# A decoder block on one core: low parts on GpSimd, two banks for the value products, scratch by key square

## The chip, the core and the metric

The kernel runs on one core of a Trainium2 chip. The core's engines work at the same time, each through its own instructions in order: TensorE (PE) multiplies matrices into the PSUM banks, with its weight loads listed apart as PEld; VectorE (DVE) and ScalarE (ACT) work on tiles in SBUF and PSUM; GpSimd (POOL) works on tiles in SBUF and issues DMAs; SyncE (SP) only issues DMAs here. Semaphores order what depends on each other. The metric is the device time of one execution in microseconds.

## The reference

One layer over 512 positions of 1024 channels, in float32. A combined projection of the normalized input gives a short gated convolution (mixer A), the queries, keys and values of an attention with three branches (mixer B), and two gates per channel:

```python
h = rmsnorm(x, norm1_g[l]); proj = h @ w_in[l]
y_a = a_b * causal_dwconv(a_c * a_x, conv_a_w[l])
y_b = nsa(q, k_cmp, v_cmp, k_sel, v_sel, k_win, v_win, gates)   # 8 heads of 64, 2 key groups
gm = jax.nn.sigmoid(g_merge)
mix = gm[..., :D_MODEL] * (y_a @ w_a_out[l]) + gm[..., D_MODEL:] * (y_b @ w_b_out[l])
x = x + mix @ w_o[l]
h = rmsnorm(x, norm2_g[l]); gu = h @ w_ffn_in[l]
g = causal_dwconv(gu[..., :D_FF], ffn_conv_w[l]) + ffn_conv_b[l]
x = x + (jax.nn.silu(g) * gu[..., D_FF:]) @ w_ffn_out[l]
```

The attention adds three softmax products, each with its gate: over 31 compressed keys, over selected key blocks, and over a window. There are 8 blocks of 64 keys and 16 may be selected, so all causal keys are; the window of 512 holds all of them too. So the selected and the window branch are both plain causal attention, each with keys and values of its own.

## The kernel before

**High and low parts.** The products have float32 accuracy out of operands of a shorter type (`F32R`): a value v becomes a high part h, which ScalarE writes by a copy (`split`, L157; the probabilities' own in L719), and a low part v - h. A product of two split operands is three matmuls: high by high, high by low, low by high. `dense` (L412 to L418) runs them over the tiles of 128 channels. The low part comes from VectorE (L158, L720), from GpSimd (L140, for the gate weights and the output weights of mixer A), or from a DMA that adds the raw weight to minus the high part (`dma_split`, L161 to L165).

**Stages.** The projections per token and the compression of keys and values come first; then attention (`attend`, L606) and, beside it, the work of mixer A (`conv_tile`, L752), the gates (`gate_tile`, L775) and mixer A's output (`mix_a_pair`, L784). Then come mixer B's output `pmb` (L838 to L851), the output projection (L876) and the feed-forward part with its down products (`ff_pair`, `down_part`).

**The order.** The program text is not the order of the engines. A planner simulates the program and lays each engine's instructions out in the order in which it expects them to be ready, the earlier text first among the ready ones. So TensorE's gate and convolution matmuls stand between those of attention, in an order that is fixed before the run. An engine that comes to an instruction whose operand isn't there waits, and all behind it wait too.

**Attention.** `attend(pt_, g, qt)` handles the four heads of group g and a query tile of 128; the calls go over query tiles 3, 2, 1, 0 and groups 0, 1 (L817 to L819). Tile qt has qt + 1 key tiles. For branch 1 (the window) and branch 0 (the selected blocks):

- *Scores.* Two matmuls per head into one of three score banks `s` (`scores`, L632). The branch-0 call has the compressed keys beside its own, except for qt = 3, which has its compressed scores in a bank `t` (`pcm`, L643).
- *Probabilities.* VectorE adds the causal mask (L686) and takes the negated maximum (L687). ScalarE writes the exponentials into the tile `e` and their sums (L688), and scales them by gate over sum (L693). For qt = 0 both branches share one `e` tile, and VectorE scales (L672). There are two `e` buffers (`NE`).
- *Turn.* `turn` (L620) brings keys onto partitions. VectorE transposes squares of 32 by 32 (L623); four DMAs on SP write them to scratch in DRAM, one for each square of 32 keys (L627); a fifth reads them back into `tn` (L629). There are two `tn` buffers (`NTN`). All waits of SP's queue hold up the weight loads behind them (L134).
- *Value products.* For each key tile ScalarE copies the high part `ph` (L719), VectorE subtracts it from `tn` in place (L720), and TensorE multiplies both with the values into the accumulator `acc` (L722, L727). Between them come the products of the compressed branch (L725), whose probabilities go through GpSimd (L703, L704) and a transposition by TensorE in a bank `t` (`ptc`, L708; read out in L713).
- *Read-out.* ScalarE and VectorE read `acc` (L729, L732); the sum is split for mixer B's output (L735, and L736 on GpSimd).

`acc` is the one bank `o`. The two banks `t` are taken in turn, whoever asks. When attention is over, its memory is given to later tiles, among them the ring of raw weights; the first load into it is that of mixer B's output weights `wr_bo` (L176), whose high part is L157.

An element of `e` before the change has its key square first, then the head, then the key in the square:

```python
return pt_.tile([P, S // SQ, HG, SQ], F32, name=name, tag="e", bufs=NE)
```

and the scratch has a 512-byte row (128 elements: 4 heads by 32 queries) as its shortest run:

```python
mid = dr.tile([QB, n, QB, SQ, P], F32, name=f"td_{e.name}", tag=f"td_{e.name}", bufs=1)
```

Of the kernel before, what the change touches and what calls it, by code (L numbers as in the profile page):

```python
# [11 lines left out]
F32 = mybir.dt.float32  # L12
F32R = mybir.dt.float32r
I32 = mybir.dt.int32
AF = mybir.ActivationFunctionType
ALU = mybir.AluOpType
AX = mybir.AxisListType

P = 128
D = 1024  # L20
S = 512
KD = D // P
NT = S // P
H = 8
G = 2
HG = H // G
# [21 lines left out]
NE = 2  # L48
# [3 lines left out]
NTN = 2  # L52
SQ = 32
QB = P // SQ
# [31 lines left out]
def tile_block(ctx: ExitStack, tc: tile.TileContext, xT, pos, par, par2, w_tok, w_a3, w_gate, w_ao, w_bo, w_o,  # L86
               w_ff, w_dn, c_w1, out):
    nc = tc.nc
    sb = ctx.enter_context(tc.tile_pool(name="sb", bufs=1, side="left"))
    dr = ctx.enter_context(tc.tile_pool(name="dr", bufs=1, space=bass.MemoryType.DRAM))  # L90
# [22 lines left out]
    def bank(tag, name, bufs):  # L113
        return ps.tile([P, 512], F32, name=name, tag=tag, bufs=bufs)
# [4 lines left out]
    def s_bank(name):  # L119
        return bank("s", name, 3)  # L120

    def t_bank(name):
        return bank("t", name, 2)

    def o_bank(name):
        return bank("o", name, 1)
# [223 lines left out]
    for t in range(NT):  # L350
        dst = a_all[:, t * 12 * HD + N_AB:(t + 1) * 12 * HD]
# [244 lines left out]
            y_all[i // 2] = pa.tile([P, 4 * TOKC], F32R, name=f"y{i // 2}", tag=f"y{i // 2}", bufs=1)  # L596
        return y_all[i // 2][:, 4 * S * (i % 2):4 * S * (i % 2 + 1)].rearrange("p (a s) -> p a s", a=4)

    def squares(v):
        return v.rearrange("p (b i) -> p b i", i=SQ)  # L600

    def by_head(v, b):

        return v.rearrange("p (q a b i) -> p a b q i", q=QB, a=2, b=2)[:, :, b]
# [1 line left out]
    def attend(pt_, g, qt):  # L606
        nk = (qt + 1) * P
# [3 lines left out]
        tag = f"{g}{qt}"  # L611
# [2 lines left out]
            pool = pxg if name in ("mx1", "mx0", "sums1") else pb if name in ("sums0", "mcs") else pt_  # L614
            return pool.tile([P, HG, n], dt, name=f"{name}{tag}", tag=name, bufs=2)

        def e_tile(name):
            return pt_.tile([P, S // SQ, HG, SQ], F32, name=name, tag="e", bufs=NE)

        def turn(e, n):  # L620

            v = e[:, 0:n * QB].rearrange("p b h i -> p (b h i)")
            nc.vector.transpose(v, v)  # L623
            v = v.rearrange("p (b r) -> p b r", r=P)
            mid = dr.tile([QB, n, QB, SQ, P], F32, name=f"td_{e.name}", tag=f"td_{e.name}", bufs=1)
            for a in range(QB):
                nc.sync.dma_start(mid[a].rearrange("k b j r -> j (k b) r"), v[a * SQ:(a + 1) * SQ])  # L627
            dst = pt_.tile([P, NT * QB, P], F32R, name=f"tn_{e.name}", tag="tn", bufs=NTN)[:, 0:n * QB]
            nc.sync.dma_start(dst.bitcast(F32), mid.rearrange("a k b j r -> (b j) (a k) r"))  # L629
            return dst.rearrange("p (a k) r -> p k a r", k=n)  # L630

        def scores(w, i, br, a, b):  # L632
            h = g * HG + i
# [6 lines left out]

        xc = small("xc", NC)
        if off == 0:
            pcm = t_bank(f"pcm{tag}").rearrange("p (h c) -> p h c", c=P)  # L643
            for i in range(HG):

                nc.tensor.matmul(pcm[:, i, 0:2 * NC], q[:, g * HG + i, :], kk[:, :, g, 0:NC], start=True, stop=True)
            nc.vector.tensor_tensor(xc, pcm[:, :, 0:NC], cm_add[:, qt, None, :].to_broadcast([P, HG, NC]), op=ALU.add)
            nc.vector.tensor_add(xc, xc, pcm[:, :, NC:2 * NC])
        acc = o_bank(f"po{tag}")
        acc4 = acc.rearrange("p (a r) -> p a r", a=QB)  # L650
        if qt == 0:

            e = e_tile(f"e{tag}")
            e4 = lambda br: e[:, br * QB:(br + 1) * QB]
            mx = pt_.tile([P, HG, 2], F32, name=f"mx{tag}", tag="mx", bufs=1)
            sums = small("sums", 2)
            for i in range(HG):
                sc = s_bank(f"sc{tag}{i}")
                w = sc[:, 0:2 * (NC + P)].rearrange("p (b k) -> p b k", b=2)
                for j in range(2):  # L660
                    nc.tensor.matmul(w, q[:, g * HG + i, :], kk5[:, j, :, g, 0:NC + P], start=j == 0, stop=j == 1)
                nc.vector.tensor_add(xc[:, i, :], w[:, 0, 0:NC], cm_add[:, qt, :])
                dg = w[:, :, NC:]
                nc.vector.tensor_tensor(dg, dg, causal[:, None, :].to_broadcast([P, 2, P]), op=ALU.add)
                nc.vector.tensor_reduce(mx[:, i], dg, axis=AX.X, op=ALU.max, negate=True)
                for br in (1, 0):
                    nc.scalar.activation(e4(br)[:, :, i], squares(dg[:, br]), AF.Exp, bias=mx[:, i, br:br + 1],
                                         accum_out=sums[:, i, br:br + 1])
            nc.vector.reciprocal(sums, sums)
            nc.vector.tensor_mul(sums, sums, gates[:, :, 1:3])  # L670
            for br in (1, 0):
                nc.vector.tensor_tensor(e4(br), e4(br), sums[:, None, :, br:br + 1].to_broadcast([P, QB, HG, SQ]), op=ALU.mult)  # L672
            turned = turn(e, 2)
        for br in (1, 0):
            if qt > 0:
                o = off if br == 0 else 0
                e = e_tile(f"e{tag}{br}")
                mx = small(f"mx{br}", 1)
                sums = small(f"sums{br}", 1)
                for i in range(HG):  # L680
                    sc = s_bank(f"sc{tag}{i}{br}")
                    scores(sc[:, 0:o + nk], i, br, NC - o, NC + nk)
                    if o:
                        nc.vector.tensor_add(xc[:, i, :], sc[:, 0:NC], cm_add[:, qt, :])
                    dg = sc[:, o + nk - P:o + nk]
                    nc.vector.tensor_add(dg, dg, causal)  # L686
                    nc.vector.tensor_reduce(mx[:, i], sc[:, o:o + nk], axis=AX.X, op=ALU.max, negate=True)  # L687
                    nc.scalar.activation(e[:, 0:nk // SQ, i], squares(sc[:, o:o + nk]), AF.Exp, bias=mx[:, i],  # L688
                                         accum_out=sums[:, i])
                scale_of(sums, 1 + br)  # L690
                for i in range(HG):
                    v = e[:, 0:nk // SQ, i]
                    nc.scalar.activation(v, v, AF.Copy, scale=sums[:, i])  # L693
                turned = turn(e, qt + 1)
            if br == 0:
                mcs = small("mcs", 2)
                mc, sc_ = mcs[:, :, 0:1], mcs[:, :, 1:2]
                nc.vector.tensor_reduce(mc[:, :, 0], xc, axis=AX.X, op=ALU.max)
                nc.vector.tensor_tensor(xc, xc, mc.to_broadcast([P, HG, NC]), op=ALU.subtract)
                nc.scalar.activation(xc, xc, AF.Exp)  # L700
                nc.vector.reduce_sum(sc_[:, :, 0], xc, axis=AX.X)
                scale_of(sc_, 0)
                nc.gpsimd.tensor_tensor(xc, xc, cm_one[:, qt, None, :].to_broadcast([P, HG, NC]), op=ALU.mult)  # L703
                nc.gpsimd.tensor_tensor(xc, xc, sc_.to_broadcast([P, HG, NC]), op=ALU.mult)  # L704
                xs = small("xs", 2 * NC, F32R)
                nc.scalar.activation(xs[:, :, 0:NC], xc, AF.Copy)
                nc.vector.tensor_sub(xs[:, :, NC:], xc, xs[:, :, 0:NC].bitcast(F32))
                pt = t_bank(f"ptc{tag}")  # L708
                for a in range(2):
                    nc.tensor.transpose(pt[:, a * P:(a + 1) * P],  # L710
                                        xs[:, 2 * a:2 * a + 2, :].rearrange("p h c -> p (h c)").bitcast(F32), ident)
                pc = pt_.tile([P, 2, P], F32R, name=f"pc{tag}", tag="pc", bufs=1)
                nc.scalar.activation(pc, pt[:, 0:2 * P].rearrange("p (a t) -> p a t", a=2), AF.Copy)  # L713
            k0 = br if qt == 0 else 0
            for kt in range(qt + 1):
                pl = turned[:, kt + k0]
                pt = pl.bitcast(F32)
                ph = pt_.tile([P, QB, P], F32R, name=f"ph{tag}{kt}{br}", tag="pth", bufs=NPT)
                nc.scalar.activation(ph, pt, AF.Copy)  # L719
                nc.vector.tensor_sub(pl, pt, ph.bitcast(F32))  # L720
                w = v_t[:, kt, 2 * br + g, :]
                nc.tensor.matmul(acc4, w, ph, start=kt == 0 and br == 1, stop=False)  # L722
                if kt == 0 and br == 0:
                    for b in range(2):
                        nc.tensor.matmul(by_head(acc, b), vc_t[:, b, g, :], pc.rearrange("p a (q i) -> p a q i", i=SQ),  # L725
                                         start=False, stop=False)
                nc.tensor.matmul(acc4, w, pl, start=False, stop=kt == qt and br == 0)  # L727
# [6 lines left out]
        dst = (slice(None), slice(2 * g, 2 * g + 2), slice(qt * P, (qt + 1) * P))  # L734
# [79 lines left out]
    pt_ = at_ctx.enter_context(tc.tile_pool(name="pt", bufs=1, side="right"))  # L814
# [23 lines left out]
    for i in range(4):  # L838
# [3 lines left out]
        w = ring_w(w_bo[i], f"bo{i}")  # L842
        for n, j in enumerate((2 * i, 2 * i + 1)):
            acc = t_bank(f"pmb{j}")
# [31 lines left out]
    for n, j in enumerate(O_ORDER):  # L876
        w = ring_w(w_o[j], f"o{j}")
        acc = d_bank(f"po_{j}")
# [8 lines left out]
        k, half = j % 4, j // 4  # L887
# [255 lines left out]
```

## Time and profile before

| | us |
|---|---|
| median of 3 runs | 720.52 |
| lowest and highest | 717.43 and 721.11 |
| the profiled execution | 720.8 |
| its span, first to last instruction | 719.1 |

| engine | busy us | share of the span |
|---|---|---|
| TensorE | 700.3 | 97% |
| weight loads | 619.9 | 86% |
| VectorE | 562.7 | 78% |
| ScalarE | 432.8 | 60% |
| GpSimd | 184.0 | 26% |

Times in the profile count from the span's start. In its rows by line stand engine, operation, output <- inputs, their shapes, the count, busy time, mean duration, and the engine's idle time ahead of them with what ended it. Matmuls overlap: the distance from one to the next is shorter than the time of one. The share of busy time is a mean over stages, so the stages are read one by one. The mean TensorE clock granted was 0.993 of the full one.

### The profile page before, as it was taken

The page shows a single profiled execution, that of the slowest core. Times are in us where ns is not written, and L with a number is a line of the kernel's source. Part 1 is how long each engine was busy: PE and PEld are TensorE (multiplying, and loading weights), DVE is VectorE, ACT ScalarE, POOL GpSimd, SP SyncE. Part 2 cuts the span into 40 slices and gives each one's busy share as a digit, 9 for nine tenths or more (in the row PEclk, how much of TensorE's full clock was granted, in tenths as well). Part 3 has the DMA queues.
Part 4 walks back from the last instruction along what each step waited for, and adds up shares of the span by engine and source line. Part 5 has one row for each costly group of instructions (what it writes and reads, how often), then busy time and mean ns, then how long its engine had stood idle before and what let it go on. Part 6 is the DMA issues. An engine that isn't in the chain of part 4 may idle for free.

```text
span 719.1 us, 11240 instructions
## 1 busy us (share of the span) xinstructions
PE 700.3 (97%) x4125; PEld 619.9 (86%) x4125; DVE 562.7 (78%) x972; ACT 432.8 (60%) x722; POOL 184.0 (26%) x179
## 2 busy tenths in 40 slices
PE   9999999988998999989999999999999999999997
PEld 9999888866877887768889999999999999999986
DVE  6887885849998899657695899997787877878643
ACT  7535655657766876533676776676654666546430
POOL 4151322222423444425012221222211122111110
PEclk9999999999999999989999999999999999999999
DMA  7333688788876675282366798987979779785675
GB/s 272 97 94 118 176 176 170 161 239 212 230 180 183 181 205 144 60 320 89 118 168 155 157 239 196 235 199 183 204 185 226 170 181 204 180 208 106 121 141 149
DMA packets 77078, 126.43 MB, mean 176 GB/s; under 512 B 5088, under 2 KB 43104, under 8 KB 77024
## 3 DMA queue, kind: packets, MB, share of 16 engines
q1 hardware_dynamic: 62464, 91.39, 41.8%
q0 software_dynamic: 14272, 34.08, 27.5%
q8 instruction: 32, 0.52, 0.3%
q10 hardware_dynamic: 288, 0.26, 0.1%
q14 instruction: 22, 0.18, 0.1%
HBM read 113.13 MB, written 12.58 MB: 175 GB/s over the span
## 4 chain that ended last, share of the span: by engine, by line
PE 81%; DVE 9%; DMA 4%; ACT 3%; issue 1%; SPq 1%; POOL 0%; ACTq 0%; DVEq 0%
PE p L416 9%; PE p L415 9%; PE p L418 9%; PE pdn L416 6%; PE pdn L415 6%; PE pdn L418 6%; DVE tn_e L720 3%; PE pa L418 2%; PE pg L416 2%; PE pg L415 2%; PE pg L418 2%; DMA td_e<-e 2%; PE po L415 2%; PE po L416 2%; PE po L418 2%; DVE e L623 2%
## 5 line engine op out<-in xcount | busy, mean ns | idle before, releaser
L416 PE MATMUL p<-xf_l,sh 128*128 128x256 f32 x336 | 80.6, 277 | 0.0
L415 PE MATMUL p<-xf_h,sh 128*128 128x256 f32 x336 | 80.6, 277 | 0.0
L416 PE MATMUL pdn<-al,wh_d 128*128 128x512 f32 x176 | 68.8, 391 | 0.0
L415 PE MATMUL pdn<-ah,wh_d 128*128 128x512 f32 x176 | 68.6, 391 | 0.0
L157 ACT ACTIVATE sh<-s 128x1024 fp32r<-128x1024 f32 x44 | 46.2, 1057 | 36.9 <-PE p L416 24.8
L416 PEld LDWEIGHTS p<-xf_l,sh 128*128 128x128 f32 x336 | 63.1, 188 | 0.1
L415 PEld LDWEIGHTS p<-xf_h,sh 128*128 128x128 f32 x336 | 63.0, 188 | 0.1
L165 POOL DMA_DIRECT2D wl_s<-in_w_ff_dram x22 | 19.5, 885 | 166.0 <-ACT wl_s L164 154.9
L158 DVE TENSOR_TENSOR sl<-s,sh 128x1024 fp32r<-128x1024 f32 x44 | 53.7, 1222 | 8.7 <-ACT sh L157 8.7
L163 ACT ACTIVATE wh_s<-wr_s 128x1024 fp32r<-128x1024 f32 x22 | 23.3, 1059 | 52.9 <-PE pdn L416 50.5
L720 DVE TENSOR_TENSOR tn_e<-tn_e,ph 128x512 fp32r<-128x512 f32 x40 | 42.7, 1070 | 15.2 <-ACT ph L719 14.9
L418 PE MATMUL p<-xf_h,sl 128*128 128x256 f32 x336 | 51.6, 277 | 0.0
L140 POOL TENSOR_TENSOR wl_g<-wr_g,wh_g 128x1024 fp32r<-128x1024 f32 x16 | 39.3, 2454 | 45.1 <-ACT wh_g L138 21.8
L415 PE MATMUL pg<-xg_h,wh_g 128*128 128x512 f32 x128 | 50.5, 394 | 0.3 <-DVE ma L792 0.3
L416 PE MATMUL pg<-xg_l,wh_g 128*128 128x512 f32 x128 | 50.3, 393 | 0.0
L418 PE MATMUL pdn<-ah,wl_d 128*128 128x512 f32 x176 | 47.7, 390 | 0.0
L165 POOL DMA_DIRECT2D wl_d<-in_w_dn_dram x22 | 26.5, 1203 | 77.2 <-ACT wl_d L164 70.0
L1062 DVE TENSOR_TENSOR x<-x,pdn 128x512 f32<-128x512 f32 x48 | 32.9, 686 | 16.2 <-PE pdn L418 15.5
L418 PEld LDWEIGHTS p<-xf_h,sl 128*128 128x128 f32 x336 | 44.5, 188 | 0.2
L415 PE MATMUL p<-xf_h,wh_s 128*128 128x256 f32 x168 | 40.5, 277 | 0.0
L416 PE MATMUL p<-xf_l,wh_s 128*128 128x256 f32 x168 | 40.5, 277 | 0.0
L688 ACT ACTIVATE e<-sc,mx 128x512 f32<-128x512 f32 (+2 forms) x48 | 27.5, 576 | 21.4 <-DVE mx L687 12.7
(360 smaller groups left out, 2115.2 us busy)
## 6 DMA issues: line engine op xcount, KB each, us to landing
wr_s<-in_w_ff_dram SPq DMA_DIRECT2D x44, 512.0 KB, 5.4
wl_s<-in_w_ff_dram POOLq DMA_DIRECT2D x22, 512.0 KB, 7.7
wr_d<-in_w_dn_dram SPq DMA_DIRECT2D x22, 512.0 KB, 6.1
wl_d<-in_w_dn_dram POOLq DMA_DIRECT2D x22, 512.0 KB, 8.4
wr_g<-in_w_gate_dram SPq DMA_DIRECT2D x16, 512.0 KB, 4.5
wr_a<-in_w_a_dram SPq DMA_DIRECT2D x12, 512.0 KB, 4.0
tl<-in_w_ff_dram POOLq DMA_DIRECT2D x22, 256.0 KB, 7.2
wl_a<-in_w_a_dram POOLq DMA_DIRECT2D x10, 512.0 KB, 7.8
```

The source lines that it names most:

```text
L140: e.tensor_sub(lo[:, 0:n], raw[:, 0:n], hi[:, 0:n].bitcast(F32))
L157: hi = nc.scalar.activation(h, v, AF.Copy)
L158: nc.vector.tensor_sub(l, v, h.bitcast(F32))
L163: nc.scalar.activation(h, raw, AF.Copy)
L165: nc.gpsimd.dma_start(l if dst is None else dst, src, accum_op=ALU.add)
L415: nc.tensor.matmul(acc, wh, xh, start=first and i == 0, stop=False)
L416: nc.tensor.matmul(acc, wh, xl, start=False, stop=False)
L418: nc.tensor.matmul(acc, wl, xh, start=False, stop=last and i == len(units) - 1)
L623: nc.vector.transpose(v, v)
L688: nc.scalar.activation(e[:, 0:nk // SQ, i], squares(sc[:, o:o + nk]), AF.Exp, bias=mx[:, i], accum_out=sums[:, i])
L720: nc.vector.tensor_sub(pl, pt, ph.bitcast(F32))
L1062: nc.vector.tensor_add(xj, xj, acc)
```

## The change

The low part of the probabilities (L720 before) is computed by GpSimd in place of VectorE. Group 1's accumulator is bank `t1` in place of `o`; `pcm` and `ptc` always take `t0`; all others alternate between `t0` and `t1`. And `e` has the key square's place in its tile of 128 first, then the key tile, then the head. The scratch follows: its rows for one key hold all key tiles one after another, so a run has n x 128 elements, n being the number of key tiles in the turn (for qt = 0 both branches count, n = 2). The bytes moved, the matmuls and the tiles' sizes are the same.

```diff
-    def t_bank(name):
-        return bank("t", name, 2)
+    n_t = []
+
+    def t_bank(name, i=None):
+        if i is None:
+            i = len(n_t) % 2
+            n_t.append(name)
+        return bank(f"t{i}", name, 1)
...
-        def e_tile(name):
-            return pt_.tile([P, S // SQ, HG, SQ], F32, name=name, tag="e", bufs=NE)
+        def e_tile(br, n):
+            return pt_.tile([P, HG * S], F32, name=f"e{tag}{br}", tag="e", bufs=NE)[:, 0:n * HG * P].rearrange(
+                "p (b k h i) -> p b k h i", b=QB, k=n, h=HG)
 
         def turn(e, n):
 
-            v = e[:, 0:n * QB].rearrange("p b h i -> p (b h i)")
+            v = e.rearrange("p b k h i -> p (b k h i)")
             nc.vector.transpose(v, v)
-            v = v.rearrange("p (b r) -> p b r", r=P)
-            mid = dr.tile([QB, n, QB, SQ, P], F32, name=f"td_{e.name}", tag=f"td_{e.name}", bufs=1)
+            w = n * P
+            dst = pt_.tile([P, HG * S], F32R, name=f"tn_{e.name}", tag="tn", bufs=NTN)[:, 0:QB * w]
+            d = dst.bitcast(F32)
+            mid = dr.tile([QB, QB, SQ, w], F32, name=f"td_{e.name}", tag=f"td_{e.name}", bufs=1)
             for a in range(QB):
-                nc.sync.dma_start(mid[a].rearrange("k b j r -> j (k b) r"), v[a * SQ:(a + 1) * SQ])
-            dst = pt_.tile([P, NT * QB, P], F32R, name=f"tn_{e.name}", tag="tn", bufs=NTN)[:, 0:n * QB]
-            nc.sync.dma_start(dst.bitcast(F32), mid.rearrange("a k b j r -> (b j) (a k) r"))
-            return dst.rearrange("p (a k) r -> p k a r", k=n)
+                nc.sync.dma_start(mid[a].rearrange("b j r -> j b r"),
+                                  v[a * SQ:(a + 1) * SQ].rearrange("p (b r) -> p b r", b=QB))
+            nc.sync.dma_start(d.rearrange("p (a r) -> p a r", a=QB), mid.rearrange("a b j r -> (b j) a r"))
+            return dst.rearrange("p (a k r) -> p a k r", a=QB, k=n)
...
-            pcm = t_bank(f"pcm{tag}").rearrange("p (h c) -> p h c", c=P)
+            pcm = t_bank(f"pcm{tag}", 0).rearrange("p (h c) -> p h c", c=P)
...
-        acc = o_bank(f"po{tag}")
+        acc = o_bank(f"po{tag}") if g == 0 else t_bank(f"po{tag}", 1)
...
-                    nc.scalar.activation(e[:, 0:nk // SQ, i], squares(sc[:, o:o + nk]), AF.Exp, bias=mx[:, i],
-                                         accum_out=sums[:, i])
+                    nc.scalar.activation(e[:, :, :, i].rearrange("p b k i -> p k b i"),
+                                         sc[:, o:o + nk].rearrange("p (k b i) -> p k b i", b=QB, i=SQ), AF.Exp,
+                                         bias=mx[:, i], accum_out=sums[:, i])
...
-                    v = e[:, 0:nk // SQ, i]
+                    v = e[:, :, :, i]
...
-                pt = t_bank(f"ptc{tag}")
+                pt = t_bank(f"ptc{tag}", 0)
...
-                pl = turned[:, kt + k0]
+                pl = turned[:, :, kt + k0]
...
-                nc.vector.tensor_sub(pl, pt, ph.bitcast(F32))
+                nc.gpsimd.tensor_sub(pl, pt, ph.bitcast(F32))
```

More of the change, by code (lines that the diff above doesn't have):

```diff
@@ L597, in y_tile @@
         return y_all[i // 2][:, 4 * S * (i % 2):4 * S * (i % 2 + 1)].rearrange("p (a s) -> p a s", a=4)
-    def squares(v):
-        return v.rearrange("p (b i) -> p b i", i=SQ)
     def by_head(v, b):
@@ L648, in attend @@
             nc.vector.tensor_add(xc, xc, pcm[:, :, NC:2 * NC])
-        acc = o_bank(f"po{tag}")
+        acc = o_bank(f"po{tag}") if g == 0 else t_bank(f"po{tag}", 1)
         acc4 = acc.rearrange("p (a r) -> p a r", a=QB)
         if qt == 0:
-            e = e_tile(f"e{tag}")
-            e4 = lambda br: e[:, br * QB:(br + 1) * QB]
+            e = e_tile("", 2)
             mx = pt_.tile([P, HG, 2], F32, name=f"mx{tag}", tag="mx", bufs=1)
@@ L666, in attend @@
                 for br in (1, 0):
-                    nc.scalar.activation(e4(br)[:, :, i], squares(dg[:, br]), AF.Exp, bias=mx[:, i, br:br + 1],
-                                         accum_out=sums[:, i, br:br + 1])
+                    nc.scalar.activation(e[:, :, br, i], dg[:, br].rearrange("p (b i) -> p b i", i=SQ), AF.Exp,
+                                         bias=mx[:, i, br:br + 1], accum_out=sums[:, i, br:br + 1])
             nc.vector.reciprocal(sums, sums)
@@ L671, in attend @@
             for br in (1, 0):
-                nc.vector.tensor_tensor(e4(br), e4(br), sums[:, None, :, br:br + 1].to_broadcast([P, QB, HG, SQ]), op=ALU.mult)
+                nc.vector.tensor_tensor(e[:, :, br], e[:, :, br],
+                                        sums[:, None, :, br:br + 1].to_broadcast([P, QB, HG, SQ]), op=ALU.mult)
             turned = turn(e, 2)
@@ L676, in attend @@
                 o = off if br == 0 else 0
-                e = e_tile(f"e{tag}{br}")
+                e = e_tile(br, qt + 1)
                 mx = small(f"mx{br}", 1)
```

## The prediction

> **What bounds the kernel now.** I read the page's first part, then the table of engine times by stretch (columns: stretch, length, then busy time and instruction count of PE, PEld, DVE, ACT and POOL, granted clock, DMA share, GB/s), cut where the attention stage begins and ends.
>
> ```profile
> span 719.1 us, 11240 instructions
> ...
> 120.00:152.00 32.00, 29.66 (x127) 24.01 (x126) 22.33 (x45) 17.74 (x35) 8.52 (x9) 0.95 0.74 178
> 152.00:306.00 154.00, 146.53 (x664) 117.93 (x663) 132.59 (x273) 107.91 (x256) 58.64 (x40) 1.00 0.68 180
> 306.00:319.00 13.00, 9.50 (x31) 7.26 (x30) 5.20 (x6) 5.33 (x7) 0.72 (x1) 0.74 0.87 301
> 319.00:719.00 400.00, 396.31 (x2670) 364.09 (x2668) 310.94 (x423) 231.59 (x303) 79.94 (x77) 1.00 0.73 176
> ```
>
> TensorE sets the time: from 319 us on it idles 3.7 of 400 us, and nothing of the change lies there. So the change is worth at most what TensorE loses between 120 and 319 us: 2.3 us idle in the first stretch, 7.5 in the second (154.00 less 146.53), 3.5 in the third, and what it loses at a lowered clock (0.95 and 0.74). In the middle stretch VectorE is 86% busy (132.59 of 154), GpSimd 38%. The waits of TensorE between 100 and 320 us name the releasers (total, times, longest):
>
> ```profile
> PE po L727 <- DVE tn_e L720: 5.3, 6, 1.5
> PE pmb L415 <- ACT wh_bo L157: 3.5, 1, 3.5
> PE sc L634 <- ACT e L688: 2.5, 2, 2.0
> ```
>
> The timeline of TensorE shows two stalls with a slow stretch behind them (start, time, line, the idle time before it and its releaser):
>
> ```profile
> 146.66 0.50 PE L634 MATMUL sc<-kk,qT 128*128 128x512 f32 x1 [2.03 <-ACT e L688]
> ...
> 151.09 0.39 PE L415 MATMUL pg<-xg_h,wh_g 128*128 128x512 f32 x1
> ...
> 306.63 1.54 PE L418 MATMUL pg<-xg_h,wl_g 128*128 128x512 f32 x6
> ```
>
> From 146.66 to 151.09 run 12 matmuls of 512 columns in 4.43 us. The last row shows their pace at full clock: six in 1.54 us, the last of them taking 0.39, so (1.54 - 0.39) / 5 = 0.23 us from one to the next. Twelve would take 2.76. So this stall costs 2.03 + 1.7 = **3.7 us**.
>
> ```profile
> 311.67 0.80 PE L415 MATMUL pmb<-y,wh_bo 128*128 128x512 f32 x1 [3.50 <-ACT wh_bo L157]
> ...
> 317.81 0.41 PE L415 MATMUL pmb<-y,wh_bo 128*128 128x512 f32 x1
> ```
>
> Here 14 matmuls take 6.14 us instead of 14 x 0.23 = 3.2: the bubble at the end of attention costs 3.5 + 2.9 = **6.4 us**. With the **7.5 us** idle between them, 17.6 us are in reach, and no more.
>
> **Part 1: the low parts go from VectorE to GpSimd (L720).** The rows by line and by tile, and of GpSimd the nearest operations:
>
> ```profile
> L720 DVE TENSOR_TENSOR tn_e<-tn_e,ph 128x512 fp32r<-128x512 f32 x40 | 42.7, 1070 | 15.2 <-ACT ph L719 14.9
> ...
> L767 POOL TENSOR_TENSOR ct<-ct,rb_n 128x512 f32<-128x512 f32 x4 | 5.1, 1277 | 7.1 <-DVE ct L747 7.1
> ...
> L140 POOL TENSOR_TENSOR wl_g<-wr_g,wh_g 128x1024 fp32r<-128x1024 f32 x16 | 39.3, 2454 | 45.1 <-ACT wh_g L138 21.8 <-PE pma L418 9.3 <-PE pg L416 8.2
> ...
> L848 POOL TENSOR_TENSOR t_all<-t_all,ma 128x512 f32<-128x512 f32 x8 | 13.9, 1742 | 18.8 <-DVE t_all L847 18.7
> ```
> ```profile
> L720 DVE TENSOR_TENSOR tn_e<-tn_e,ph x40: 644/682/2908, 153.3 to 300.3; 128x512 fp32r<-128x512 f32 x40
> ```
>
> The median subtraction takes 0.68 us, the mean 1.07: 42.7 - 40 x 0.682 = 15.4 us are delay. One of the long ones beside GpSimd's timeline:
>
> ```profile
> 163.62 2.39 POOL L140 TENSOR_TENSOR wl_ao<-wr_ao,wh_ao 128x1024 fp32r<-128x1024 f32 x1 [5.01 <-ACT wh_ao L138]
> ```
> ```profile
> 163.85 2.71 DVE L720 TENSOR_TENSOR tn_e<-tn_e,ph 128x512 fp32r<-128x512 f32 x1
> ```
> ```profile
> 166.61 0.51 PE L727 MATMUL po<-tn_e,v_t 128*128 128x512 f32 x1 [1.06 <-DVE tn_e L720]
> ```
>
> The subtraction starts 0.2 us after GpSimd's and ends 0.55 us after it: it stood still while GpSimd ran, and TensorE paid 1.06 us. VectorE loses 42.7 us in the stretch and falls to 89.9 of 154 (58%). GpSimd gains 40 x 1.277 = 51.1 us (bounds 1.277 free, 1.742 in L848: 51 to 70) and rises to 109.7 (71%), or 128 (83%). I take 1.277, since that row runs beside the same VectorE work. The standing still now falls on VectorE's remaining subtractions and products of two SBUF tiles, such as this one, which handles four elements in each partition and took 2.10 us:
>
> ```profile
> 251.04 2.10 DVE L639 TENSOR_TENSOR sums<-sums,gate_n 128x4 f32<-128x4 f32 x1
> ```
>
> By the program there are 42 of these (20 in L639, 2 in L670, 4 in L672, 8 each in L699 and L707). A GpSimd engine that is 71% busy with instructions of about 1.28 us holds each up by 0.71 x 0.64 = 0.45 us, 19 us in all (bounds 0 and 42 x 1.28 = 54), of which those behind L140 are paid already. VectorE still comes out near 70%, so it stops being the second bound.
>
> GpSimd works in order. The subtraction waits for ScalarE's high part (L719), and behind it queue L140 (the low weights that the gate products L418 read), L703 and L704 (compressed probabilities) and L736; it queues behind them too. No DMA stands in its way: the last one that GpSimd issues in this stage comes before the first subtraction (153.3 in the tile's row):
>
> ```profile
> 134.42 0.86 POOL L165 DMA_DIRECT2D wl_a<-in_w_a_dram  x1 [3.37 <-ACT wl_a L164]
> ```
>
> What it costs when the cover goes: the step itself gets 0.60 us longer (1.277 - 0.682), and one that meets an L140 waits up to 2.45 us, which is what the standing still costs today. The idle 7.5 us is therefore not all won. I take half, **3.7 us** (bounds: all 7.5; a loss, in the rivals).
>
> [...] The rows give 1277/682 = 1.87. [...]
>
> **Part 2: key square by key square in scratch.** VectorE's transpose has the same 128 partitions and elements. The exponential's write gets one more stride, with runs of 32 as before:
>
> ```profile
> L688 ACT ACTIVATE e<-sc,mx 128x512 f32<-128x512 f32 x16 | 10.9, 684 | 10.3 <-DMA td_e<-e 6.7 <-DVE mx L687 3.6
> ...
> L693 ACT ACTIVATE e<-e,sums 128x512 f32<-128x512 f32 x16 | 10.3, 713 | 0.5 <-DVE sums L639 0.5
> ```
>
> L693, which reads and writes in such runs, takes 0.03 us more than L688; between 0 and 48 x 0.03 = 1.4 us of ScalarE, which is 70% busy there (107.91 of 154), I take 0, and ScalarE's idle time would hide the rest. Scratch runs grow from 512 B to n x 512 B, n being the key tiles. Over the 14 turns n adds up to 40, so packets go from 40 x 1024 = 40,960 to 14 x 1024 = 14,336, of queue q1's 62,464; bytes stay.
>
> ```profile
> td_e<-e SPq DMA_DIRECT2D x16, 256.0 KB, 5.0
> ...
> out_dram<-x SPq DMA_DIRECT2D x8, 256.0 KB, 2.0
> ```
> ```profile
> q1 hardware_dynamic: 62464, 91.39, 41.8%
> ```
>
> The output's write has the same size in runs of 2 KB, as the new scratch write has at n = 4: 2.0 us against 5.0 (bounds 2.0 and 5.0; I take near 2.0, the row with equal size and runs). The chain of waits shows where this is on the path:
>
> ```profile
> 131.54 0.33 SPq L627
> ...
> 134.72 11.00 DMA td_e<-e
> 145.83 0.79 ACT e L688 x2
> ```
>
> The first scratch write lands 11 us after its issue; until then the probability buffer isn't free, ScalarE's exponential waits, the score banks stay full and TensorE stalls 2.03 us. Only 2.03 of those 11 us need go for the **3.7 us** of stall and slow clock to vanish. I take all of it. Elsewhere an earlier landing only adds slack.
>
> [...]
>
> **Part 3: the value products alternate between banks.** Group 0 keeps bank o, group 1 takes t1, and the transposed compressed probabilities keep t0 alone: eight uses in the stage, each free again after one ScalarE copy, so nothing:
>
> ```profile
> 293.60 0.36 ACT L713 ACTIVATE pc<-ptc 128x256 fp32r<-128x256 f32 x1
> ```
>
> What it frees is the last products, which today wait until the previous group's sums are read out:
>
> ```profile
> 299.06 1.90 DVE L720 TENSOR_TENSOR tn_e<-tn_e,ph 128x512 fp32r<-128x512 f32 x2 [2.16 <-ACT ph L719]
> 300.88 0.84 DVE L732 TENSOR_TENSOR yo<-po,yt 64x256 f32<-64x256 f32 x2
> ```
> ```profile
> 305.48 0.39 PE L722 MATMUL po<-ph,v_t 128*128 128x512 f32 x1
> ...
> 306.39 0.40 PE L727 MATMUL po<-tn_e,v_t 128*128 128x512 f32 x1
> ```
> ```profile
> 306.87 1.78 SPq L176 DMA_DIRECT2D wr_bo<-in_w_bo_dram  x4
> ```
> ```profile
> 310.56 1.06 ACT L157 ACTIVATE wh_bo<-wr_bo 128x1024 fp32r<-128x1024 f32 x1 [0.74 <-DMA wr_bo<-in_w_bo_dram]
> ```
>
> The last low part is ready at 300.96, the bank at 301.72, and the products run at 305.48 because the order puts a gate product in front. The next weights' load waits for the last of them (their memory is freed then) and needs 311.67 - 306.79 = 4.9 us up to the first matmul. Were the last product at about 302, load and split would lie behind gate work that lasts until 308.17 (306.63 + 1.54 above), and the bubble would go. But the planner sets the place anew: I take half of the 6.4, **3.2 us** (bounds 0 and 6.4).
>
> **Sum.** The profiled run took 720.8 us with a span of 719.1, 1.7 around it; the median of the runs shown is 720.52. 3.7 + 3.7 + 3.2 = 10.6, so 720.8 - 10.6 = **710.2 us**. About 0.5% is what a measurement can tell from no change: under 717 is faster, over 724 slower.
>
> **Rivals.**
> 1. All 17.6 us go: 703.2 us. For it: VectorE at 58% leaves the chain slack everywhere. Against: small idle times remain in any order laid out ahead. Chance 0.06.
> 2. The scratch writes are no faster, their 11 us being due to other traffic (DMA share 0.74 in that stretch). The first stall stays: 713.9 us. [...] Chance 0.12.
> 3. The waits change names: TensorE waits for GpSimd where it waited for VectorE, the order moves the stalls, the bubble remains. For it: half of TensorE's idle time is where the planned order meets a late operand, and the order is planned anew. 718 to 723 us, about 720. Chance 0.22.
> 4. GpSimd's queue becomes the bound. Today 15.4 us of delay in L720 cost TensorE 5.3, a third. On GpSimd the delay is 40 x 0.60 = 24 us, and 19 instructions of 2.45 us (the table of stretches has 46.65 us for L140 below) stand in front of a subtraction each: 47 more. A third of 71 is 24 us, 19 more than now; less 3.7 and 3.2 that is 12 us: 733 us. To be slower by over 0.5% TensorE must wait 10.5 us more than now, 15.8 in all, 47 us of delay, so about ten of the nineteen must stand ahead of a needed low part: (47 - 24) / 2.45 = 9.6. For it: GpSimd is 71 to 83% busy and in order. Against: the order of each engine's work is laid out ahead with this queue in it, while the standing still comes on top of today's order. [...] Chance 0.20.
>
> ```profile
> 152.00:306.00 154.00, 0.00 (x0) 46.65 (x19) 1.00 0.68 180
> ```
>
> My forecast, 705 to 716 us, has the other 0.40. Faster: 0.40 + 0.06 + 0.12 = 0.58; same 0.22; slower 0.20. The range leaves out the slower rival alone: 702 to 724.
>
> **What would show it.** L720 as 40 GpSimd instructions near 1.28 us; VectorE near 60 to 70% between the first and last of them; the q1 packets near 35,800 and the 256 KB scratch write near 2 us; no wait of a score product near 146 us; the last L727 followed by several us of gate products, and no slow clock at the first pmb. I am wrong if TensorE waits for GpSimd's L720 for more than 5.3 us in all, if the first scratch write still takes some 11 us, or if the wait for wh_bo stays at 3.5.

## The result, and the profile after

The changed kernel takes **711.94 us** (median of 4 runs, 710.54 to 714.02) against 720.58 (4 runs): a ratio of 0.9882, 95% interval 0.9858 to 0.9906. On another occasion, beside other kernels, it took 710.80 us, ratio 0.9877 (0.9860 to 0.9894). The forecast was 710.2.

The table of engine times by stretch, at the cuts used before the change (busy time of PE, PEld, DVE, ACT, POOL, then granted clock, DMA share, GB/s):

```profile
120.00:152.00 32.00, 30.64 (x137) 24.49 (x136) 24.98 (x49) 19.87 (x37) 7.25 (x8) 1.00 0.72 172
152.00:306.00 154.00, 146.45 (x669) 118.93 (x668) 116.72 (x238) 111.55 (x260) 110.27 (x82) 1.00 0.67 205
306.00:319.00 13.00, 13.00 (x59) 10.78 (x58) 8.09 (x10) 4.43 (x6) 6.03 (x4) 1.00 0.26 85
```

The 13 us behind attention have lost their idle time (3.5 us before) and their low clock (0.74 before). The middle is as idle as it was: 154.00 - 146.45 = 7.55 us against 7.47. GpSimd has gone from 58.64 to 110.27 us there, VectorE from 132.59 to 116.72. The waits of TensorE between 100 and 330 us show that the middle's idle time has other names now:

```profile
PE ptc L716 <- DVE xs L713: 3.9, 2, 2.0
PE sc L639 <- ACT e L693: 2.0, 4, 1.1
PE po L728 <- ACT ph L725: 1.8, 2, 1.3
PE ptc L716 <- DVE xc L666: 0.7, 1, 0.7
```

No wait for a low part (L726 now) or for wh_bo is left. The subtraction by line, from the page, and the end of attention from the timelines of TensorE and of SP's queue:

```profile
L726 POOL TENSOR_TENSOR tn_e<-tn_e,ph 128x512 fp32r<-128x512 f32 x40 | 52.0, 1311 | 30.7 <-ACT ph L725 29.9
```
```profile
294.14 0.39 PE L733 MATMUL po<-tn_e,v_t 128*128 128x512 f32 x1
294.37 0.39 PE L421 MATMUL pg<-xg_l,wh_g 128*128 128x512 f32 x1
...
302.53 0.39 PE L420 MATMUL pmb<-y,wh_bo 128*128 128x512 f32 x1
302.76 0.39 PE L421 MATMUL pmb<-y,wh_bo 128*128 128x512 f32 x1
```
```profile
294.56 1.76 SPq L181 DMA_DIRECT2D wr_bo<-in_w_bo_dram  x4
```

The last value product is at 294.14 us where it was at 306.39. The next weights' load starts right behind it, and gate matmuls without a gap cover load and split. The scratch is another matter:

```profile
td_e<-e SPq DMA_DIRECT2D x16, 256.0 KB, 5.4
```
```profile
q1 hardware_dynamic: 41984, 91.39, 40.5%
```
```profile
137.73 10.25 DMA td_e<-e
```

Packets in q1 fell by a third, but the 256 KB write lands in 5.4 us (5.0 before), the queue takes 40.5% of the DMA engines' time (41.8% before), and the first write still takes 10.25 us in the chain of waits.

This profile has one disturbance that the profile before lacks, ahead of attention:

```profile
81.79 3.65 PE L423 MATMUL pa<-xg_h,wl_a 128*128 128x512 f32 x8 [1.86 <-DMA wl_a<-in_w_a_dram]
85.24 0.46 PE L420 MATMUL pa<-xg_h,wh_a 128*128 128x512 f32 x1
```

Eight matmuls take 3.45 us to the next instead of 8 x 0.23 = 1.84, so it costs 1.86 + 1.6 = 3.5 us. TensorE's order is the same in both kernels up to 137 us, and TensorE waits no more than 0.5 us for this load in any other profile, the changed kernel's second included: the stall belongs to this one execution, not to the change. The second profile (after_again below, span 711.2 us) is therefore the better one to read the stretches from:

```profile
120.00:152.00 32.00, 28.36 (x126) 22.51 (x125) 24.42 (x47) 18.55 (x37) 7.27 (x9) 1.00 0.74 188
290.00:320.00 30.00, 30.00 (x135) 24.85 (x134) 16.24 (x18) 11.24 (x15) 13.04 (x9) 1.00 0.47 158
```

At the start of attention it idles 3.64 us at full clock, where the kernel before idled 2.34 us and lost 1.7 us to the slow clock: 0.4 us are won there. At the end of attention nothing is idle or slow any more.

### The profile page after: what moved, and what is told of

The parts are those of the page before. It is cut to its first block, busy times and chain, and to the rows that moved or that the text cites. A ratio compares the mean times of both kernels' runs of the same rounds, so it can differ in the third digit from the quotient of the medians.

```text
span 712.3 us, 11270 instructions
## 1 busy us (share of the span) xinstructions
PE 696.3 (98%) x4125; PEld 617.6 (87%) x4125; DVE 544.1 (76%) x932; ACT 432.4 (61%) x722; POOL 234.3 (33%) x219
## 3 DMA queue, kind: packets, MB, share of 16 engines
q1 hardware_dynamic: 41984, 91.39, 40.5%
## 4 chain that ended last, share of the span: by engine, by line
PE 85%; DVE 6%; DMA 4%; ACT 3%; POOL 1%; issue 1%; SPq 0%; ACTq 0%; DVEq 0%
PE p L421 9%; PE p L420 9%; PE p L423 9%; PE pdn L421 6%; PE pdn L420 6%; PE pdn L423 6%; PE pg L421 3%; PE pg L420 3%; PE pg L423 2%; PE pa L423 2%; PE po L420 2%; PE po L421 2%; PE po L423 2%; PE pa L420 2%; PE pa L421 2%; PE pj_s L264 2%
## 5 line engine op out<-in xcount | busy, mean ns | idle before, releaser
L726 POOL TENSOR_TENSOR tn_e<-tn_e,ph 128x512 fp32r<-128x512 f32 x40 | 52.0, 1311 | 30.7 <-ACT ph L725 29.9
L145 POOL TENSOR_TENSOR wl_g<-wr_g,wh_g 128x1024 fp32r<-128x1024 f32 x16 | 38.4, 2398 | 8.5 <-PE pa L423 6.1
L420 PE MATMUL p<-xf_h,wh_s 128*128 128x256 f32 x168 | 40.5, 276 | 0.0
L421 PE MATMUL p<-xf_l,wh_s 128*128 128x256 f32 x168 | 40.5, 276 | 0.0
L423 PEld LDWEIGHTS pdn<-ah,wl_d 128*128 128x128 f32 x176 | 33.0, 188 | 6.9
```

Of the source, the lines that this page charges most:

```text
L145: e.tensor_sub(lo[:, 0:n], raw[:, 0:n], hi[:, 0:n].bitcast(F32))
L420: nc.tensor.matmul(acc, wh, xh, start=first and i == 0, stop=False)
L421: nc.tensor.matmul(acc, wh, xl, start=False, stop=False)
L423: nc.tensor.matmul(acc, wl, xh, start=False, stop=last and i == len(units) - 1)
L726: nc.gpsimd.tensor_sub(pl, pt, ph.bitcast(F32))
```

## The experiments

The three parts were taken alone and in pairs, each on its own kernel. Ratios are to the kernel before, timed beside each; the last columns are TensorE's waits in us, from each kernel's profile: for the next weights (wh_bo), for the compressed probabilities' transposition (ptc), and for a low part of the probabilities.

| kernel | low part by | acc banks | scratch by | us | ratio, 95% interval | wh_bo | ptc | low part |
|---|---|---|---|---|---|---|---|---|
| before | VectorE | 1 | head | 720.58 | | 3.5 | 1.1 | 5.3 |
| sub_only | GpSimd | 1 | head | 714.77 | 0.9918 (0.9897 to 0.9940) | 3.0 | 0.9 | 0 |
| banks_only | VectorE | 2 | head | 721.81 | 1.0024 (1.0013 to 1.0036) | 0.6 | 3.2 | 2.8 |
| scratch_only | VectorE | 1 | square | 718.16 | 0.9971 (0.9960 to 0.9982) | 3.7 | 1.0 | 6.0 |
| no_scratch | GpSimd | 2 | head | 715.51 | 0.9929 (0.9914 to 0.9944) | 0 | 4.7 | 0 |
| no_sub | VectorE | 2 | square | 716.90 | 0.9962 (0.9950 to 0.9974) | 1.8 | 3.2 | 2.2 |
| no_banks | GpSimd | 1 | square | 710.08 | 0.9855 (0.9832 to 0.9878) | 2.6 | 0.3 | 0 |
| after_again | GpSimd | 2 | square | 710.80 | 0.9877 (0.9860 to 0.9894) | 0 | 4.6 | 0 |

**sub_only.**

```diff
-                nc.vector.tensor_sub(pl, pt, ph.bitcast(F32))
+                nc.gpsimd.tensor_sub(pl, pt, ph.bitcast(F32))
```

> Only the subtraction goes to GpSimd; banks and scratch as before. Theory A, the bubble at the end of attention goes only if the last value product comes early enough, and that takes both the free engine and the second bank: here 9 gate matmuls stand behind the last value product (6 before, 36 after the change), 9 x 0.227 = 2.0 of the 4.9 us that load and split of the next weights take, so the wait for wh_bo falls from 3.5 to about 2.9 us and most of the slow clock stays; 717 to 721 us. Theory B, the freed VectorE alone carries the gain: the wait for wh_bo is gone and the time near 712. Theory C, GpSimd in order costs more than it frees: TensorE waits for L720 more than 5.3 us and the time is above 721.

```profile
PE pmb L415 <- ACT wh_bo L157: 3.0, 1, 3.0
PE po L722 <- ACT ph L719: 2.6, 2, 1.7
PE po L722 <- DVE yo L732: 2.2, 1, 2.2
```

In TensorE's waits the bubble is there as theory A had it (3.0, expected 2.9), but the time is 714.77, below A's range: A left out the waits for the low part, 5.3 us, and these are all gone. Their 5.3 us are not simply the gain, though: waits for ph and yo, 4.8 us, have taken most of their place. Of the 6.2 us between the spans of the two profiles 3.4 come from the clock: the trace before has 3.4 us at half clock behind the first stall and 6.8 us at the end of attention, this one 3.4 us in all. C falls. B falls too: the part is worth more than half of the change's gain, not all. Its largest new wait, 2.2 us, is for the read-out of the one bank (yo).

**banks_only.**

```diff
-        acc = o_bank(f"po{tag}")
+        acc = o_bank(f"po{tag}") if g == 0 else t_bank(f"po{tag}", 1)
```

with the alternation of `t0` and `t1` as in the change.

> Only the second accumulator bank. Theory A: 15 gate matmuls stand behind the last value product, 3.4 of 4.9 us, so the wait for wh_bo falls from 3.5 to about 1.5 us; 715 to 719 us. Theory D, the bank alone carries the gain: the wait is gone and the time near 712. If the bank does nothing: 720.

```profile
PE po L727 <- ACT ph L724: 3.9, 4, 1.8
PE ptc L715 <- DVE xs L712: 3.2, 2, 1.8
PE sc L639 <- ACT e L693: 2.9, 1, 2.9
PE po L732 <- DVE tn_e L725: 2.8, 4, 1.1
PE pma L420 <- DVE ma L784: 0.6, 1, 0.6
PE pmb L420 <- ACT wh_bo L162: 0.6, 1, 0.6
```

The wait for wh_bo shrinks, even below theory A's 1.5 us, and the kernel is still slower by 0.24%: waits for ptc, for high parts and for scores have taken the place. Neither A nor D holds.

**scratch_only** and **no_scratch**: the `e_tile`, `turn` and exponential lines of the change alone, and the change without them.

> Only the scratch by key square. Prediction's term: the 256 KB write lands in about 2 us instead of 5.0 and the stall of the score product near 146 us goes: 716 to 717 us. Rival, the runs of 512 B were long enough: landing 5 us as before, the stall of about 2 us stays, 720 us.

> Subtraction on GpSimd and second bank, scratch as before the change. Theory A: 36 gate matmuls behind the last value product, no wait for wh_bo, 710 to 713 us, as with the whole change. If the longer runs carry 3.7 us of the gain: 714 to 716 us.

The DMA issues and the timeline of TensorE in scratch_only:

```profile
td_e<-e SPq DMA_DIRECT2D x16, 256.0 KB, 5.3
```
```profile
146.12 0.50 PE L634 MATMUL sc<-kk,qT 128*128 128x512 f32 x1 [1.19 <-ACT e L688]
...
151.87 0.50 PE L723 MATMUL po<-ph,v_t 128*128 128x512 f32 x1 [0.69 <-ACT ph L720]
```

The time is between the two expectations (718.16), and the write lands no earlier, as the rival had it: the 256 KB write takes 5.0 to 5.2 us in the four profiles with scratch by head, and 5.2 to 6.8 us in six with scratch by square (5.3 in this one, 5.4 and 5.2 in the two of the whole change). Still the part gains 0.29%. In this profile the first stall is 1.19 + 0.69 us with no slow stretch between, where the kernel before had 3.7 with its slow stretch: 1.8 us, near the 2.1 that 0.29% makes. With GpSimd's part it is worth more: no_scratch has a ratio of 0.9929 against 0.9877, and sub_only 0.9918 against no_banks 0.9855, 3.7 and 4.5 us. The profiles of no_scratch and after_again show 1.3 us of it in the first stalls (2.75 + 1.86 against 2.02 + 1.28 us); where the rest comes from is open.

**no_sub, no_banks, after_again.**

> Bank and scratch of the change, the subtraction back on VectorE. Theory A: 15 gate matmuls behind the last value product, a wait for wh_bo near 1.5 us, L720's mean again near 1.07 us on VectorE, 715 to 719 us. If GpSimd's part is worth nothing: 712.

> Subtraction on GpSimd and scratch of the change, one accumulator bank. Theory A: 10 gate matmuls behind the last value product, a wait for wh_bo near 2.6 us, 716 to 720 us. If the bank is worth nothing: 712.

> The changed kernel once more, beside the next ones on the same chip. 710 to 713 us. The profiled run of it had a stall of 1.9 us with a slow stretch near 82 us, in a part where the order of all engines is that of the kernel before; if that is chance of the single execution, this profile lacks it and its span is some 3 us shorter than 712.3; if the change causes it, it is here again.

no_sub lands in its range (716.90; wait for wh_bo 1.8). no_banks does not: 710.08 us with a wait for wh_bo of 2.6 us as expected, and still as fast as the whole change (0.9832 to 0.9878 against 0.9860 to 0.9894). **Within the change the second bank is worth nothing measurable**, though it does away with the bubble. What pays for it is the wait for ptc, 0.3 us against 4.6.

The table holds four pairs of kernels for each part that differ in this part alone. GpSimd's part gains 0.8 to 1.2% in each of them, and the scratch 0.3 to 0.6%. The second bank moves the time by -0.1 to +0.2%.

VectorE's and GpSimd's timelines in after_again show where the wait for ptc comes from:

```profile
278.94 1.87 DVE L713 TENSOR_TENSOR xs<-xc,xs 128x128 fp32r<-128x128 f32 x1
```
```profile
278.30 2.36 POOL L145 TENSOR_TENSOR wl_g<-wr_g,wh_g 128x1024 fp32r<-128x1024 f32 x1
```
```profile
L713 DVE TENSOR_TENSOR xs<-xc,xs x8: 273/892/2242, 132.2 to 278.9; 128x128 fp32r<-128x128 f32 x8
```

The same row of the kernel before:

```profile
L707 DVE TENSOR_TENSOR xs<-xc,xs x8: 270/284/2324, 132.5 to 295.1; 128x128 fp32r<-128x128 f32 x8
```

The subtraction of 128 x 128 elements takes 0.27 us at best (first of the three times), 0.89 in the median (0.28 before) and 2.24 at worst. In the first two rows it starts 0.6 us after GpSimd's and ends 0.15 us after it, at 280.81, and the transposition waits 2.01 us for it. It is the standing still that L720 had before, one instruction further on. So this subtraction went to GpSimd as well.

**xs_pool.**

```diff
-                nc.vector.tensor_sub(xs[:, :, NC:], xc, xs[:, :, 0:NC].bitcast(F32))
+                nc.gpsimd.tensor_sub(xs[:, :, NC:], xc, xs[:, :, 0:NC].bitcast(F32))
```

> The whole change, and the low part of the compressed probabilities (xs, 128 x 128 elements) by GpSimd too. In the changed kernel TensorE waits 3.9 us, in two waits, for ptc, held up by that subtraction on VectorE, which stands still while GpSimd runs. If the standing still is the cause, the two waits go and the time falls by 2 to 4 us to 708 to 710; if the chain behind them is late anyway, other waits take their place and the time stays at 711 to 713.

**704.87 us, ratio 0.9788 (0.9774 to 0.9801)**, faster than both kernels. Its waits between 60 and 330 us:

```profile
PE sc L639 <- ACT e L693: 2.4, 1, 2.4
PE po L728 <- ACT ph L725: 2.2, 2, 1.3
PE pg L420 <- DVE ma L798: 0.3, 1, 0.3
```

The waits for ptc are gone, and that for wh_bo is not back. The gain, 6 us, is above the 2 to 4 expected: besides the 3.9 us of waits there were 0.7 us of a third wait for ptc, and about 1.5 us of slow matmuls behind one of them in after_again (shown at the end). The granted clock is 1.0 in all five runs of xs_pool and 0.995 to 0.998 in the eight of the changed kernel. The subtraction itself is not ready sooner, as GpSimd's timeline shows for the same place:

```profile
278.65 2.39 POOL L145 TENSOR_TENSOR wl_g<-wr_g,wh_g 128x1024 fp32r<-128x1024 f32 x1
280.99 0.46 POOL L713 TENSOR_TENSOR xs<-xc,xs 128x128 fp32r<-128x128 f32 x1
```

It stands behind L145 in the queue instead of standing still beside it, and ends at 281.45. But now the order of TensorE has the transposition later, with gate matmuls ahead of it. That the planner reckons with a queue and not with the standing still would explain this; it is argued, not tested. Since TensorE's order differs too, the gain cannot be put down to the standing still alone.

**xs_nobanks, xs_half, xs_e0, xs_conv**, all with xs_pool's edit. The first has one accumulator bank. xs_half gives every other key tile's subtraction back to VectorE:

```diff
-                nc.gpsimd.tensor_sub(pl, pt, ph.bitcast(F32))
+                (nc.vector if kt % 2 else nc.gpsimd).tensor_sub(pl, pt, ph.bitcast(F32))
```

xs_e0 takes the scaling of the probabilities to ScalarE, one instruction for each head:

```diff
-                nc.vector.tensor_tensor(e[:, :, br], e[:, :, br],
-                                        sums[:, None, :, br:br + 1].to_broadcast([P, QB, HG, SQ]), op=ALU.mult)
+                for i in range(HG):
+                    v = e[:, :, br, i]
+                    nc.scalar.activation(v, v, AF.Copy, scale=sums[:, i, br:br + 1])
```

xs_conv gives the split of one more weight ahead of attention to VectorE:

```diff
-            w = load_w(w_a3[2 + 3 * i + j], D, f"a{i}{j}", by="dma" if 3 * i + j > 1 else "vector")
+            w = load_w(w_a3[2 + 3 * i + j], D, f"a{i}{j}", by="dma" if 3 * i + j > 2 else "vector")
```

> xs_pool with one accumulator bank again. The runs so far: the second bank takes away the wait for wh_bo (2.6 and 3.0 us without it, 0 with it and GpSimd's part), but the time did not fall, since waits for ptc came (0.3 to 0.9 us without it, 3.9 with it). Theory: the bank is worth the bubble at the end of attention, some 3 to 5 us, as soon as xs no longer stands still; then this is 707 to 710 us, with a wait for wh_bo of 2 to 3.5 us. Rival: the bank only moves waits about; then 703 to 706 us, like xs_pool.

> xs_pool with the subtractions of odd key tiles (16 of 40) back on VectorE. If standing still against GpSimd is the cost: the 16 take 0.9 us and more in the mean instead of 0.68, TensorE waits for them again for 1 to 3 us, 706 to 710 us. Rival, GpSimd's queue of 72% is what now holds the chain: 702 to 704 us.

> xs_pool, and for query tile 0 the scaling of the probabilities by ScalarE (as for the other tiles) in place of VectorE's product of two SBUF tiles, which stands still against GpSimd. If that lies on the path: the waits near 263 us (1 us) go, 703 to 705 us. If ScalarE's eight instructions cost more than they free: 705 to 707 us.

> xs_pool, and the first convolution weight that is split by a DMA from GpSimd's queue is split by VectorE instead. In one of ten profiles so far that DMA stood behind a long instruction of GpSimd and TensorE lost some 3.4 us near 82 us. If it is that rare, the median moves by less than 0.5 us from xs_pool's 704.9, and the spread gets smaller; if VectorE's 1.2 us more there delays attention, 705 to 707 us.

| kernel | us | ratio, 95% interval | wh_bo | ptc | low part |
|---|---|---|---|---|---|
| xs_pool | 704.87 | 0.9788 (0.9774 to 0.9801) | 0 | 0 | 0.2 |
| xs_nobanks | 708.16 | 0.9828 (0.9809 to 0.9847) | 3.3 | 0 | 0 |
| xs_half | 713.04 | 0.9910 (0.9889 to 0.9932) | 0 | 0.9 | 2.7 |
| xs_e0 | 704.23 | 0.9789 (0.9764 to 0.9813) | 0 | 0 | 0 |
| xs_conv | 710.39 | 0.9867 (0.9850 to 0.9885) | 0 | 0.3 | 0.6 |

xs_nobanks bears out its theory: with xs out of the way the second bank is worth 0.0040 of the time, 2.9 us, and the bubble is what it takes away:

```profile
300.71 0.50 PE L415 MATMUL pmb<-y,wh_bo 128*128 128x512 f32 x1 [3.34 <-ACT wh_bo L157]
```

xs_half is 8 us slower than xs_pool, more than expected. The groups by line show why the sharing fails:

```profile
L726 POOL TENSOR_TENSOR tn_e<-tn_e,ph 128x512 fp32r<-128x512 f32 x24 | 33.4, 1395 | 22.1 <-ACT ph L725 21.9 <-DVE mcs L644 0.3
...
L726 DVE TENSOR_TENSOR tn_e<-tn_e,ph 128x512 fp32r<-128x512 f32 x16 | 23.1, 1446 | 7.9 <-ACT ph L725 7.5 <-issue 0.3
```

On VectorE the 16 take 1.45 us in the mean, twice the undisturbed 0.68 and longer than GpSimd's own. So GpSimd's queue was not what held the chain. In the changed kernel the four scalings that xs_e0 takes from VectorE took 0.68 to 0.95 us, so they stood still for at most 0.27 us each. xs_e0 is as fast as xs_pool; in its profile the 1.0 us wait near 263 us is gone, but the times do not tell the two kernels apart. xs_conv costs 5.5 us where nothing to 2 us was expected; its profile has 5.5 us of waits for high parts (L725) and none near 82 us. TensorE's order differs from xs_pool's from 79 us on; whether this or VectorE's one longer split has the effect was not tested. It is a warning for the other comparisons: an edit outside attention moved the time by more than most parts are worth, and every edit has the order planned anew. GpSimd's part and the scratch have four pairs each behind them; the second bank's 2.9 us have one pair and the wait that went.

## Why the prediction was right, point by point

**The bound.** Right: nothing behind 319 us changed, and the gain of 8.6 us came out of the 17.6 in reach.

**Part 1, 3.7 us.** The part pays more than forecast, and not where it was to. L720's work takes 1.311 us on GpSimd (1.277 forecast), of TensorE's 5.3 us of waits for it at most 0.6 are left in any kernel that gives all 40 to GpSimd, and alone it gains 0.82%, 5.9 us. But the 3.7 us were to come out of the middle's idle time, and with the whole change that is as long as before (7.55 us against 7.47): 4.6 us of waits for ptc have taken the place. GpSimd's busy time came out as worked out (110.27 against 109.7). VectorE's was estimated at about 70% and is 116.72 of 154, 76%. The rival of waits that only change names (720 us) is right about the middle and wrong about the time. The rival of GpSimd's queue (733 us) did not happen; what it says of the instruction is true of its duration (1.311 us in the mean against a median of 0.682 on VectorE) and did not decide.

**Part 2, 3.7 us.** This step failed. "I take near 2.0, the row with equal size and runs" was the wrong row: run length was not what made the scratch write slow (5.0 us with runs of 512 B, 5.4 with runs of 2 KB). The output's write also comes at the kernel's end and from 128 partitions where the scratch's comes from 32; which of these counts was not tested. The scratch write stayed at 5.4 us, and the first one at 10.25, which the prediction had named as a sign of being wrong. Packets fell by 20,480, not 26,624. By the packet sizes in the traces the scratch takes 14,336 now, as worked out, but it took 34,816 before, not 40,960: 32,768 of 512 B and the rest of 2 KB already. What the part gives by itself, 2.1 us, fits a first stall that is 0.8 us shorter and has no slow stretch behind it. With the whole change the first stall of after_again is 2.02 us again, and whether a slow stretch follows goes, in these traces, with where the stall falls (last section). So it stays open what the part's gain in all four pairs comes from.

**Part 3, 3.2 us.** The mechanism is right, its net in this change nothing. The last products came early, load and split lay behind gate matmuls, and all 6.4 us of bubble went. It took Part 1 as well: the wait for wh_bo is 0.6 and 1.8 us with the bank and without GpSimd's part, 3.0 and 2.6 the other way round, and 0 with both. But with two banks the order let TensorE meet the compressed branch too early, and the standing still of xs, which Part 1 had put at 19 us over all such instructions and left out of the sum, cost 3.9 us of waits. By xs_pool and xs_nobanks, the bank is worth 2.9 us once that is removed.

So that the sum, 10.6 us, came near the 8.6 measured is in good part luck. Place by place the bubble gave all of its 6.4 us where 3.2 were forecast, the first stall about 0.4 of 3.7 (by after_again), and the middle's idle time nothing of 3.7. Part by part, GpSimd's part gave more than its term, the scratch gained without its mechanism, and the bank's gain was paid back in the middle.

## What to carry to other kernels

Where long VectorE instructions of two inputs end just after GpSimd's, as L720 and then L713 did here (2.71 us against a median of 0.68, 1.87 against 0.27 at best), suspect that they stood still; the price can move on to the next such instruction when one is taken away. Look at the largest time of each line beside its smallest, and move all of those on the path, not half. And a part that shows no gain, like the second bank, may only be hidden behind another wait: read which wait took its place before dropping it. Where the order of all engines is planned anew with every edit, take a part on and off in several kernels before giving it a price.

## What the runs showed of the hardware

**The clock behind a stall.** An idle gap of 2.03 us in the kernel before was followed by 3.4 us at half clock (147.2 to 150.6). A longer one in no_scratch was not, as the timeline of its TensorE shows:

```profile
146.30 0.50 PE L639 MATMUL sc<-kk,qT 128*128 128x512 f32 x1 [2.75 <-ACT e L693]
...
149.63 0.39 PE L420 MATMUL pg<-xg_h,wh_g 128*128 128x512 f32 x1
149.86 0.39 PE L421 MATMUL pg<-xg_l,wh_g 128*128 128x512 f32 x1
```

The matmuls of 149.63 and 149.86 are 0.23 us apart, the full pace. The two executions of the changed kernel show it best, at the same place of the same order, behind gaps of the same length. First the one with the whole table above, then after_again:

```profile
283.63 0.41 PE L716 MATMUL ptc<-ident,xs 128*128 128x128 f32 x2 [2.02 <-DVE xs L713]
283.79 1.64 PE L423 MATMUL pg<-xg_h,wl_g 128*128 128x512 f32 x6
285.27 0.39 PE L420 MATMUL pg<-xg_h,wh_g 128*128 128x512 f32 x1
```
```profile
280.96 0.66 PE L716 MATMUL ptc<-ident,xs 128*128 128x128 f32 x2 [2.01 <-DVE xs L713]
281.27 2.91 PE L423 MATMUL pg<-xg_h,wl_g 128*128 128x512 f32 x6
283.97 0.52 PE L420 MATMUL pg<-xg_h,wh_g 128*128 128x512 f32 x1
```

From the transposition to the last of these rows it is 1.64 us in the one and 3.01 in the other. So the length of the gap alone does not decide, and the same stall of 2 us may cost 2 us or some 3.5.

What goes with it in these traces is the place of the gap. The granted clock changes in steps of 3.413 us: in the trace of the kernel before, its stretches last 139.9 us at 1.0, 3.4 at 0.5, 160.4 at 1.0 and 6.8 at 0.5, which is 41, 1, 47 and 2 steps; in the first of the changed kernel 75.1 us at 1.0, 3.4 at 0.5 and 628.1 at 1.0, which is 22, 1 and 184. Cut at these steps, from 60 us to the last matmuls, the 11 traces with a stretch at 0.5 in that time agree: behind each of the 14 steps at full clock in which TensorE idles 1.77 us or more the granted clock is 0.5, and behind none in which it idles 1.75 us or less. banks_only has both of these: its gap of 1.77 us, up to 308.70, is followed by a slow step, and its gap of 1.75 us, up to 275.47, is not. After_again's gap has 1.87 us in one step; the other execution's is divided, 1.74 and 0.28 us, and no_scratch's 2.75 us into 1.60 and 1.16. What sets the 3.413 us and the limit between 1.75 and 1.77 us, and whether they hold in another kernel, no run shows.
